# Four copies of 32 row-fetched tokens instead of three of 42, and weighed activations two pairs of tiles ahead

## The chip, the cores and the metric

The kernel runs on one core of one Trainium2 chip. Its time is the device time of one execution in microseconds (us). Each kernel is executed several times, and the median is compared.

## What is computed

The reference is one layer of a stream encoder on 272 tokens (16 learned ones and 256 of the input): a layer norm, two kinds of attention, an output projection, and at the end a feed-forward part (PEER) that holds two thirds of the time. For each of the 256 input tokens PEER picks 128 of 16384 one-neuron experts and sums them:

```
h = layer_norm(ALPHA * h + mix, ln1_g[l], ln1_b[l])
...
s1, i1 = lax.top_k(s[:, :, 0], P_TOPK)
s2, i2 = lax.top_k(s[:, :, 1], P_TOPK)
...
g = jax.nn.softmax(top, axis=-1).reshape(P_BLOCK, P_HEADS * P_TOPK)
act = jax.nn.gelu(jnp.einsum('td,tkd->tk', xb, u_tab[eidx]))
return jnp.einsum('tk,tkd->td', g * act, v_tab[eidx])
```

`u_tab` and `v_tab` are 16384 rows of 2048 numbers each, in float32: 134 MB per table, in HBM.

## The kernel before

PEER is done in two ways at once, and the tokens are divided between them. The **dense tokens** (NT = 214 of the 256) go through all 16384 experts on TensorE; experts that were not picked get the weight 0. The other NS = 42 tokens are **row-fetched**: for each expert that such a token picked, its row of the table is fetched by an indirect DMA, and VectorE does the sums. G = 3 copies of the 42 tokens stand on 126 partitions, and each copy takes a third of the 128 experts, so that K = 43 fetches of `u_tab` and 43 of `v_tab` (126 rows of 8 KB each, 1.03 MB) do for all of them.

The tables come in half tiles of 128 x 1024 (512 KB, called units here). `load_half` (line 128) puts a unit into one of four buffers `raw` from SyncE's queue (SP); `split_half` rounds it to `wh` on ScalarE (L134) and makes the remainder `wl` on VectorE (L137). There are four buffers of each. `begin()` starts the next unit, three ahead of the one that TensorE reads, and a unit's load waits until its buffer has been read by L137.

Stage **U** loops over 128 tiles of `u_tab` (two units each). Every tile makes 16 products for the dense tokens, each of two matmuls: 214 columns with `wl` (L1114) and 2 x 214 = 428 columns with `wh` (L1115); the first product of a tile has three (L1110 to L1112). After a tile, the generator `activation` takes its sum from PSUM in steps, four steps to a tile: a copy on ScalarE (L1055), a sum on VectorE (L1057), a pause, then the gelu on ScalarE (L1068 into `slots` for the first HELD = 74 tiles, L1073 into `ya` and from there to the DRAM array `ad` for the others). In the same stage GpSimd scatters the experts' weights into the DRAM array `gd` (L957, 256 indirect DMAs).

Stage **V** loops over the 128 tiles of `v_tab`, once for each half of the columns (h = 0, 1), one unit at a time, 8 products to a unit (`value`, same lines L1114 and L1115). Its moving operand is `wv`, the weighed activations of a pair of tiles, made by `weigh(i)` in three steps: times `gd` on VectorE (L1094), rounded on ScalarE (L1097), the remainder on VectorE (L1099). For h = 1 the first step is left out where the product is still in SBUF, for tiles up to `far` = HELD + LATE. While TensorE reads pair i, `weigh(i+1)` is issued at products 0, 3 and 6 of the pair's first unit. When it ends, `fetch_weights(i+2)` asks for the pair's part of `gd` (214 KB) on ScalarE's DMA queue, into the buffer (one of two) that was just read.

In both stages `sparse(rate)` lets the row-fetched tokens on: it adds 2 x rate to a credit, and each credit pays for one fetch (`fetch_row`, L1031, on GpSimd) or for one use of a fetched buffer (`use_row`: L1018 in the first table, L1025 in the second, on VectorE). Rates are 0.36 in U, once a tile from tile 28 on, and 0.2 in V, once a unit. There are two buffers, and each fetch waits until its buffer has been used.

TensorE, VectorE, ScalarE and SP work strictly in the order in which these loops are written; nothing reorders it in U and V.

Of the kernel before, what the change touches and what calls it, by code (L numbers as in the profile page):

```python
# [19 lines left out]
P = 128  # L20
# [4 lines left out]
L = NM + S  # L25
# [8 lines left out]

G = 3
NS = P // G
# [3 lines left out]

HELD, LATE = 74, 40

# [5 lines left out]
def hybrid_layer(ctx: ExitStack, tc: tile.TileContext, a: dict):  # L48
# [578 lines left out]
    def use_ckv(wh, wl):  # L627
        ps = project(wh, wl, hT, 0, L)
        hi = g.tile([P, L], F32R, name="ckh", tag="vwh", bufs=2)
        lw = g.tile([P, L], F32R, name="ckl", tag="vwl", bufs=2)  # L630
        nc.scalar.copy(out=hi, in_=ps)
        nc.vector.tensor_tensor(out=lw, in0=ps, in1=hi.bitcast(F32), op=ALU.subtract)
        ck.append((hi, lw))
        step()
# [426 lines left out]
    def activation(j, ps):  # L1061

        x = tmp()[:, :NT]
        yield from gather_out(two(ps), x)
        yield
        yield
        if j < HELD:
            nc.scalar.activation(out=slots[:, j], in_=x, func=AF.Gelu_apprx_tanh)  # L1068
            return
        k = (j - HELD) % 4  # L1070
        if k == 0:
            spill[:] = [g.tile([P, 4, NT], F32, name="ya", tag="wv", bufs=2)]
        nc.scalar.activation(out=spill[0][:, k], in_=x, func=AF.Gelu_apprx_tanh)  # L1073
        if k == 3 or j == P - 1:
            nc.scalar.dma_start(out=ad[:, j - HELD - k:j - HELD + 1], in_=spill[0][:, :k + 1])
# [13 lines left out]
    def weigh(i):  # L1089
        h, m = divmod(i, P // 2)  # L1090
        j = 2 * m
        x = slots[:, j:j + 2] if j < HELD else late[0][:, j - HELD:j - HELD + 2] if j < far else ring[m % 2]
        if h == 0 or j >= far:
            nc.vector.tensor_tensor(out=x, in0=x, in1=gts[m % 2], op=ALU.mult)  # L1094
            yield
        w = g.tile([P, 2, 2, NT], F32R, name="wv", bufs=2)
        nc.scalar.copy(out=w[:, :, 0], in_=x)  # L1097
        yield
        nc.vector.tensor_tensor(out=w[:, :, 1], in0=x, in1=w[:, :, 0].bitcast(F32), op=ALU.subtract)  # L1099
        wv[m] = w  # L1100
        fetch_weights(i + 2)
# [14 lines left out]

    def value(pv, wh, wl, j, d):
        ds_ = slice(d * P, (d + 1) * P)
        product(pv[d], wh[:, ds_], wl[:, ds_], wv[j // 2][:, j % 2], j == 0, j == P - 1)

# [54 lines left out]
    for n in range(2 * P):  # L1175
# [11 lines left out]
        for k in range(KT // 2):  # L1187
            kt, ks = i * KT // 2 + k, slice(k * P, (k + 1) * P)
            product(ps, wh[:, ks], wl[:, ks], hT[:, kt, :, :NT], kt == 0, kt == KT - 1)
            if k % 4 == 3:  # L1190
                q = 2 * i + k // 4
                if q == 3:
                    sparse(0.36 if j >= 28 else 0)
                if q == 3 or (q == 1 and (j % 8 or j < 28)):
                    scatter_some(1)
                step()
        if n == 2 * P - 2:
            whole_of(weigh(0))
    drain()
    whole_of(activation(P - 1, ps))  # L1200
    over = g.tile([P, KT * 2 * L], F32, name="over", tag="actT")
# [6 lines left out]
    for lo in range(0, LATE, 8):  # L1208
        later.append((16 + lo // 2, late[0][:, lo:lo + 8], ad[:, lo:lo + 8]))
    for t in range(2):  # L1210
# [7 lines left out]
    for h in range(2):  # L1218
        pv = [psum() for _ in range(8)]
        for j in range(P):  # L1220
# [8 lines left out]
            w = got.popleft()  # L1229
            if j % 2 == 0 and h * P + j < 2 * P - 2:  # L1230
                stage = weigh((h * P + j) // 2 + 1)
            for d in range(8):
                value(pv, *w, j, d)
                if j % 2 == 0 and d in (0, 3, 6) and stage:
                    next(stage, None)
                if d == 4:
                    sparse(0.2)
        if h == 0:
# [47 lines left out]
    for d in range(8):  # L1286
        value(pv, *w, P - 1, d)
        whole_of(gather_out(two(pv[d]), res[:, 8 + d, :NT]))
# [82 lines left out]
```

## Time and profile before

| | us |
|---|---|
| median of 3 runs (lowest to highest) | 2107.59 (2090.7 to 2110.59) |
| the profiled execution, its own time | 2106.06 |
| its span in the trace | 2104.3 |

The profile is of one execution; 1.8 us of its time lie outside the span. A busy time of PE (TensorE) is not TensorE at its peak: matmuls overlap, and an instruction's duration is longer than the distance to the next. Where a stage is to be priced, the distance of starts counts. "PEclk" is the granted clock as a share of 2.4 GHz; 1.2 GHz is the only other level. "DMA" is the mean busy share of 16 DMA engines.

### The profile page before, as it was taken

How to read it: one execution, taken by the hardware profiler on the slowest of the kernel's cores; microseconds unless marked ns; L12 is line 12 of the kernel's file. 1: busy time of each engine (PE TensorE's matmuls, PEld its weight loads, DVE VectorE, ACT ScalarE, POOL GpSimd, SP SyncE). 2: the span in 40 equal slices, each digit the busy share in tenths (PEclk: the TensorE clock that was granted, in tenths of full speed). 3: DMA queues.
4: the chain of work that ended last, by engine and by line, in shares of the span. 5: the costliest groups of instructions: out<-in, count | busy, mean ns of one | idle time of the engine just before them, and what ended most of it. 6: DMA issues, size and time to landing. Idle time of an engine off the chain costs nothing.

```text
span 2104.3 us, 32423 instructions
## 1 busy us (share of the span) xinstructions
PE 1910.5 (91%) x12376; PEld 1799.4 (86%) x12376; DVE 1463.7 (70%) x2193; ACT 976.0 (46%) x1458; POOL 676.5 (32%) x402
## 2 busy tenths in 40 slices
PE   7889998998999988999999998988999889998885
PEld 5888998887999978988989897878888779988784
DVE  7564577556879889756667665766777767766567
ACT  5443454534456555444545453444444445443432
POOL 3000003003588806777877673100100101101001
PEclk9999999999999999999999999999999989999997
DMA  6995443553768868999999999898888868899881
GB/s 191 272 251 178 161 159 137 181 191 122 210 181 207 210 205 244 263 251 261 288 280 298 259 310 283 284 321 277 297 294 295 293 226 279 282 294 267 274 293 52
DMA packets 186636, 506.08 MB, mean 241 GB/s; under 512 B 54534, under 2 KB 84366, under 8 KB 173838
## 3 DMA queue, kind: packets, MB, share of 16 engines
q1 hardware_dynamic: 115312, 370.96, 54.6%
q0 software_dynamic: 52256, 98.06, 19.5%
q10 hardware_dynamic: 18912, 34.99, 4.8%
q8 instruction: 97, 1.59, 0.3%
q14 instruction: 59, 0.48, 0.1%
HBM read 477.62 MB, written 25.16 MB: 239 GB/s over the span
## 4 chain that ended last, share of the span: by engine, by line
DMA 28%; PE 18%; DVE 15%; issue 8%; ACT 6%; ACTq 1%; POOL 0%; DVEq 0%; SPq 0%
DMA raw<-u_tab 14%; DMA raw<-v_tab 11%; PE ps L1115 9%; DVE wl L137 7%; ACT wh L134 5%; PE ps L1114 4%; DMA mem<-gd 2%; PE ps L181 1%; PE ps L180 1%; PE ps L179 1%; DVE tmp L1057 1%; DVE wv L1099 1%; DVE mem L1025 1%; DVE mem L1018 1%; DMA raw<-w_pq 1%
## 5 line engine op out<-in xcount | busy, mean ns | idle before, releaser
L137 DVE TENSOR_TENSOR wl<-raw,wh 128x1024 fp32r<-128x1024 f32 x660 | 809.0, 1231 | 490.7 <-ACT wh L134 473.4
L134 ACT CAST wh<-raw 128x1024 fp32r<-128x1024 f32 x666 | 695.4, 1049 | 734.1 <-DMA raw<-u_tab 195.0
L1115 PE MATMUL ps<-wv,wh 128*128 128x428 f32 x2032 | 658.5, 385 | 33.2 <-DVE wv L1099 33.0
L1115 PE MATMUL ps<-actT,wh 128*128 128x428 f32 x1920 | 606.0, 373 | 0.0
L1114 PE MATMUL ps<-wv,wl 128*128 128x214 f32 x2032 | 546.0, 269 | 40.5 <-ACT wv L1097 40.5
L1114 PE MATMUL ps<-actT,wl 128*128 128x214 f32 x1920 | 509.7, 265 | 26.7 <-DVE wl L137 26.6
L957 POOL DMA_INDIRECT gd<-mem x256 | 479.5, 1873 | 85.6 <-issue 75.3
L1115 PEld LDWEIGHTS ps<-wv,wh 128*128 128x128 f32 x2032 | 397.1, 195 | 58.6 <-DVE wv L1099 42.0
L1114 PEld LDWEIGHTS ps<-wv,wl 128*128 128x128 f32 x2032 | 404.1, 199 | 47.3 <-ACT wv L1097 47.2
L1114 PEld LDWEIGHTS ps<-actT,wl 128*128 128x128 f32 x1920 | 369.6, 193 | 33.6 <-DVE wl L137 33.2
L1115 PEld LDWEIGHTS ps<-actT,wh 128*128 128x128 f32 x1920 | 364.3, 190 | 14.7
L179 PE MATMUL ps<-actT,wh 128*128 128x256 f32 (+1 forms) x944 | 278.4, 295 | 4.9 <-ACT actT L350 4.9
L180 PE MATMUL ps<-actT,wh 128*128 128x256 f32 (+1 forms) x944 | 272.7, 289 | 4.6 <-POOL actT L229 4.4
L181 PE MATMUL ps<-actT,wl 128*128 128x256 f32 (+1 forms) x944 | 271.4, 288 | 0.5 <-DVE wl L137 0.5
L1031 POOL DMA_INDIRECT mem<-v_tab,mem x43 | 58.8, 1368 | 565.2 <-DVE mem L1025 506.7
L179 PEld LDWEIGHTS ps<-actT,wh 128*128 128x128 f32 x944 | 182.7, 194 | 12.6 <-ACT actT L350 5.2
L180 PEld LDWEIGHTS ps<-actT,wh 128*128 128x128 f32 x944 | 182.3, 193 | 7.4 <-POOL actT L229 6.1
L181 PEld LDWEIGHTS ps<-actT,wl 128*128 128x128 f32 x944 | 182.0, 193 | 0.7 <-DVE wl L137 0.7
L1031 POOL DMA_INDIRECT mem<-u_rows,mem x43 | 63.1, 1467 | 230.7 <-DVE mem L1018 201.3
L1097 ACT CAST wv<-mem 128x428 fp32r<-128x428 f32 x88 | 48.3, 548 | 124.0 <-DVE mem L1094 118.8
L1025 DVE SCALAR_TENSOR_TENSOR mem<-mem 126x2048 f32<-126x2048 f32 x42 | 98.5, 2346 | 0.0
L1018 DVE CUSTOM_DVE_ANT_0 mem<-mem 126x2048 f32<-126x2048 f32 x43 | 98.2, 2285 | 0.0
(281 smaller groups left out, 1634.7 us busy)
## 6 DMA issues: line engine op xcount, KB each, us to landing
raw<-u_tab SPq DMA_DIRECT2D x256, 512.0 KB
raw<-v_tab SPq DMA_DIRECT2D x256, 512.0 KB
raw<-w_in SPq DMA_DIRECT2D x86, 512.0 KB
raw<-w_out SPq DMA_DIRECT2D x32, 512.0 KB
raw<-w_pq SPq DMA_DIRECT2D x32, 512.0 KB
mem<-gd ACTq DMA_DIRECT2D x71, 214.0 KB
gd<-mem SPq DMA_DIRECT2D x16, 856.0 KB
ad<-ya ACTq DMA_DIRECT2D x13, 428.0 KB
```

The source lines that it names most:

```text
L134: acts.append(order(nc.scalar.copy(out=wh, in_=raw)))
L137: subs.append(order(nc.vector.tensor_tensor(out=wl, in0=raw, in1=wh.bitcast(F32), op=ALU.subtract)))
L179: nc.tensor.matmul(out, wh, ah, start=first, stop=False)
L180: nc.tensor.matmul(out, wh, al, start=False, stop=False)
L181: nc.tensor.matmul(out, wl, ah, start=False, stop=last)
L957: s = nc.gpsimd.indirect_dma_start(out=gdf[:, :], out_offset=bass.IndirectOffsetOnAxis(ap=idx, axis=0), in_=val, in_offset=None, compute_o ...
L1018: nc.vector.tensor_tensor_reduce(out=buf[:U], in0=buf[:U], in1=xsp[:U], scale=1.0, scalar=0.0, op0=ALU.mult, op1=ALU.add, accum_out=sact[: ...
L1025: nc.vector.scalar_tensor_tensor(out=xsp[:U], in0=buf[:U], scalar=sw[:U, k:k + 1], in1=xsp[:U], op0=ALU.mult, op1=ALU.add)
L1031: f = nc.gpsimd.indirect_dma_start(out=buf[:U], out_offset=None, in_=a["u_rows" if n < K else "v_tab"], in_offset=bass.IndirectOffsetOnAxi ...
L1097: nc.scalar.copy(out=w[:, :, 0], in_=x)
L1114: nc.tensor.matmul(lo, wl, x[:, 0], start=False, stop=False)
L1115: nc.tensor.matmul(two(ps)[:, :, :NT], wh, x, start=False, stop=last)
```

## The change

It does three things. First, G goes from 3 to 4: 32 tokens are row-fetched, on 4 x 32 = 128 partitions, 32 fetches per table, and 224 tokens are dense. HELD and LATE become 70 and 38 (the buffers' bytes), and the rates become 0.33 and 0.14. Second, `wv` has three buffers instead of two, is kept by the pair's running number i, and `weigh(i+2)` is issued where `weigh(i+1)` was; the first two pairs are weighed ahead of V. To make room, two small tiles of an early stage share the buffers of `wv`. Third, `activation` pauses for two steps more, half a tile, ahead of the gelu.

```
-G = 3
+G = 4
...
-HELD, LATE = 74, 40
+HELD, LATE = 70, 38
...
         yield from gather_out(two(ps), x)
-        yield
-        yield
+        for _ in range(4):
+            yield
...
-        w = g.tile([P, 2, 2, NT], F32R, name="wv", bufs=2)
+        w = g.tile([P, 2, 2, NT], F32R, name="wv", bufs=3)
...
-        wv[m] = w
+        wv[i] = w
...
-                    sparse(0.36 if j >= 28 else 0)
+                    sparse(0.33 if j >= 28 else 0)
...
         if n == 2 * P - 2:
             whole_of(weigh(0))
+        if n == 2 * P - 1:
+            whole_of(weigh(1))
     drain()
+    while beside:
+        step()
...
-            if j % 2 == 0 and h * P + j < 2 * P - 2:
-                stage = weigh((h * P + j) // 2 + 1)
+            if j % 2 == 0:
+                i = (h * P + j) // 2 + 2
+                stage = weigh(i) if i < P else None
...
-                    sparse(0.2)
+                    sparse(0.14)
```

On ScalarE (ACT), in the middle of U, one tile stood like this before (numbers are those of the buffers; the copy and the gelu of one tile have neighbouring `tmp` numbers):

```order
L1055 COPY tmp_13217<-ps_13151 128x214
L134 CAST wh_13230<-raw_13228 128x1024
L1073 ACTIVATE ya_13198<-tmp_13216 128x214
L134 CAST wh_13253<-raw_13251 128x1024
L1055 COPY tmp_13268<-ps_13206 128x214
```

and stands like this now:

```order
L1055 COPY tmp_13208<-ps_13142 128x224
L1073 ACTIVATE ya_13218<-tmp_13152 128x224
L134 CAST wh_13223<-raw_13221 128x1024
L134 CAST wh_13246<-raw_13244 128x1024
L1055 COPY tmp_13261<-ps_13197 128x224
L1073 ACTIVATE ya_13218<-tmp_13207 128x224
```

Before, the gelu of a tile (`tmp_13216`) stood behind the copy of the same tile (`tmp_13217`), one cast later; now it stands behind the copy of the next tile (`tmp_13207` behind `tmp_13261`), ahead of both casts.

On ScalarE at the end of U and the start of V, before:

```order
L1055 COPY tmp_13375<-ps_13309 128x214
L1097 CAST wv_13387<-mem_76 128x2x214
L1085 DMA mem_76<-gd_289 128x428
L134 CAST wh_13393<-raw_13391 128x1024
L1073 ACTIVATE ya_13413<-tmp_13374 128x214
L1055 COPY tmp_13416<-ps_13362 128x214
L1073 ACTIVATE ya_13413<-tmp_13415 128x214
L1075 DMA ad_290<-ya_13413 128x428
L134 CAST wh_13432<-raw_13430 128x1024
L1097 CAST wv_13449<-mem_76 128x2x214
```

and now:

```order
L1097 CAST wv_13382<-mem_76 128x2x224
L1085 DMA mem_76<-gd_289 128x448
L134 CAST wh_13388<-raw_13386 128x1024
L1097 CAST wv_13410<-mem_76 128x2x224
L1085 DMA mem_76<-gd_289 128x448
L1073 ACTIVATE ya_13414<-tmp_13367 128x224
L1055 COPY tmp_13417<-ps_13355 128x224
L1073 ACTIVATE ya_13414<-tmp_13416 128x224
L1075 DMA ad_290<-ya_13414 128x448
L134 CAST wh_13433<-raw_13431 128x1024
L1097 CAST wv_13450<-mem_76 128x2x224
```

One more pair is weighed ahead of the last tile's copy (L1055), so that the cast in V's first unit is that of the third pair and no longer of the second; from there on each is a pair earlier. The distance from a fetch of `gd` (L1085) to the cast behind the product that reads it is two pairs, as before.

On GpSimd (POOL) from the last scatters to the end of V, before:

```order
L957 DMA gd<-mem 4194304x1 x3
L1031 DMA mem<-u_rows,mem 126x2048 x8
L1031 DMA mem<-v_tab,mem 126x2048 x30
L1226 MEMSET mem 128x16x42
L1031 DMA mem<-v_tab,mem 126x2048 x13
```

and now:

```order
L957 DMA gd<-mem 4194304x1 x5
L1031 DMA mem<-v_tab,mem 128x2048 x27
L1230 MEMSET mem 128x16x32
L1031 DMA mem<-v_tab,mem 128x2048 x5
```

After the last scatter 51 fetches followed before, and 32 do now; all fetches of `u_rows` (the row layout of `u_tab`) stand between the scatters.

## Rows read from the trace of the kernel before

**Rows 1.** The page: the span, the busy times of the engines, and the DMA engines' busy share in 40 slices of the span, in tenths.

```profile
span 2104.3 us, 32423 instructions
PE 1910.5 (91%) x12376; PEld 1799.4 (86%) x12376; DVE 1463.7 (70%) x2193; ACT 976.0 (46%) x1458; POOL 676.5 (32%) x402
...
DMA  6995443553768868999999999898888868899881
```

**Rows 2.** The instructions of line 1110, the first matmul of a sum: 128 tiles of U, then 16 sums of V, with the first and last start.

```profile
L1110 PE MATMUL ps<-actT,wh x128: 261/261/381, 607.8 to 1293.4; 128*128 128x214 f32 x128
L1110 PE MATMUL ps<-wv,wh x16: 418/545/547, 1304.9 to 1706.9; 128*128 128x214 f32 x16
```

**Rows 3.** What TensorE waited for most in U (607 to 1305 us): total us, times, longest.

```profile
PE ps L1114 <- DVE wl L137: 26.6, 22, 3.6
```

**Rows 4.** What TensorE waited for in V (1305 to 2062 us), all of it.

```profile
PE ps L1114 <- ACT wv L1097: 40.5, 24, 5.6
PE ps L1115 <- DVE wv L1099: 33.0, 38, 1.9
PE ps L1110 <- DVE tmp L1057: 7.8, 8, 3.4
PE ps L1110 <- ACT wv L1097: 6.4, 1, 6.4
```

**Rows 5.** The table by stretches: length, busy us and instructions of PE, weight loads, VectorE, ScalarE and GpSimd, then the granted clock, the DMA share and GB/s. Four stretches of U, both halves of V, all of V, and one short stretch of V for PE's line 1115 alone.

```profile
607.00:700.00 93.00, 93.00 (x627) 90.71 (x626) 84.99 (x229) 54.58 (x87) 80.20 (x43) 1.00 0.80 199
700.00:850.00 150.00, 134.95 (x863) 127.76 (x861) 135.78 (x339) 80.40 (x134) 75.46 (x46) 0.99 0.80 225
850.00:1000.00 150.00, 140.00 (x904) 133.75 (x903) 97.04 (x105) 71.23 (x110) 111.00 (x61) 0.99 0.92 256
1000.00:1250.00 250.00, 240.24 (x1560) 231.23 (x1560) 163.42 (x175) 123.73 (x188) 192.91 (x108) 0.99 1.00 286
...
1305.00:1707.00 402.00, 351.30 (x2078) 330.54 (x2078) 285.64 (x301) 169.06 (x205) 34.34 (x26) 0.93 0.88 290
1707.00:2062.00 355.00, 324.18 (x1990) 310.50 (x1991) 242.43 (x220) 158.57 (x188) 33.46 (x24) 0.95 0.85 270
...
1305.00:2062.00 757.00, 675.47 (x4067) 641.05 (x4068) 528.08 (x521) 327.63 (x393) 67.79 (x50) 0.94 0.86 281
...
1350.00:1400.00 50.00, 40.94 (x132) 24.57 (x131) 0.98 0.98 323
```

**Rows 6.** The timeline of PE in V: the first and the last of 27 matmuls of line 1114 with no wait between them (start, us).

```profile
1480.10 0.26 PE L1114 MATMUL ps<-wv,wl 128*128 128x214 f32 x1
...
1488.08 0.26 PE L1114 MATMUL ps<-wv,wl 128*128 128x214 f32 x1
```

**Rows 7.** The chain of work in U: the second matmuls of two tiles that follow one another with no wait (start, us).

```profile
1103.16 0.11 PE ps L1111
...
1108.10 0.11 PE ps L1111
```

**Rows 8.** The timeline of PE in V, from a wait on.

```profile
1650.22 0.73 PE L1115 MATMUL ps<-wv,wh 128*128 128x428 f32 x1 [1.78 <-DVE wv L1099]
1650.74 0.38 PE L1114 MATMUL ps<-wv,wl 128*128 128x214 f32 x1
...
1651.32 0.38 PE L1114 MATMUL ps<-wv,wl 128*128 128x214 f32 x1
```

**Rows 9.** The timeline of PE in an early stage: the first and last of 36 matmuls of 256 columns, and of 74 of 272 columns, each with no wait between.

```profile
209.84 0.29 PE L180 MATMUL ps<-actT,wh 128*128 128x256 f32 x1
...
214.00 0.28 PE L179 MATMUL ps<-actT,wh 128*128 128x256 f32 x1
...
235.81 0.29 PE L179 MATMUL ps<-actT,wh 128*128 128x272 f32 x1
...
244.97 0.29 PE L180 MATMUL ps<-actT,wh 128*128 128x272 f32 x1
```

**Rows 10.** The page's groups of the remainder and the cast of a unit, and of the fetched rows' uses on VectorE, and from the table of lines from 570 us on that of the weighing's product: busy us in total, mean ns of one.

```profile
L137 DVE TENSOR_TENSOR wl<-raw,wh 128x1024 fp32r<-128x1024 f32 x660 | 809.0, 1231 | 490.7 <-ACT wh L134 473.4
L134 ACT CAST wh<-raw 128x1024 fp32r<-128x1024 f32 x666 | 695.4, 1049 | 734.1 <-DMA raw<-u_tab 195.0
...
L1025 DVE SCALAR_TENSOR_TENSOR mem<-mem 126x2048 f32<-126x2048 f32 x42 | 98.5, 2346 | 0.0
...
L1094 DVE TENSOR_TENSOR mem<-mem 128x428 f32<-128x428 f32 x51 | 30.5, 598 | 4.3 <-DMA mem<-gd 2.9 <-DMA mem<-ad 1.4
```

**Rows 11.** What the other engines waited for, in U (700 to 1330 us) the first two, in V (1330 to 2060 us) the others.

```profile
ACT wh L134 <- DMA raw<-u_tab: 193.3, 88, 6.3
ACT mem L1068 <- DVE tmp L1057: 53.1, 36, 3.3
...
ACT wh L134 <- DMA raw<-v_tab: 111.9, 62, 7.4
ACT wv L1097 <- DVE mem L1094: 107.4, 46, 4.3
```

**Rows 12.** The chain of work in V: transfers that it passes through (start, us from the step before to the landing).

```profile
1399.91 11.58 DMA mem<-gd
...
1491.42 10.46 DMA mem<-gd
...
1524.11 9.02 DMA raw<-v_tab
```

More of the change, by code (lines that the diff above doesn't have):

```diff
@@ L628, in use_ckv @@
         ps = project(wh, wl, hT, 0, L)
-        hi = g.tile([P, L], F32R, name="ckh", tag="vwh", bufs=2)
-        lw = g.tile([P, L], F32R, name="ckl", tag="vwl", bufs=2)
+        both = g.tile([P, 2, L], F32R, name="ckv", tag="wv", bufs=3)
+        hi, lw = both[:, 0], both[:, 1]
         nc.scalar.copy(out=hi, in_=ps)
@@ L1071, in activation @@
         if k == 0:
-            spill[:] = [g.tile([P, 4, NT], F32, name="ya", tag="wv", bufs=2)]
+            spill[:] = [g.tile([P, 4, NT], F32, name="ya", tag="wv", bufs=3)]
         nc.scalar.activation(out=spill[0][:, k], in_=x, func=AF.Gelu_apprx_tanh)
@@ L1115, in product, with value @@
             nc.tensor.matmul(two(ps)[:, :, :NT], wh, x, start=False, stop=last)
-    def value(pv, wh, wl, j, d):
+    def value(pv, wh, wl, j, d, h):
         ds_ = slice(d * P, (d + 1) * P)
-        product(pv[d], wh[:, ds_], wl[:, ds_], wv[j // 2][:, j % 2], j == 0, j == P - 1)
+        product(pv[d], wh[:, ds_], wl[:, ds_], wv[(h * P + j) // 2][:, j % 2], j == 0, j == P - 1)
     def affines():
@@ L1208, in hybrid_layer @@
     for lo in range(0, LATE, 8):
-        later.append((16 + lo // 2, late[0][:, lo:lo + 8], ad[:, lo:lo + 8]))
+        later.append((16 + lo // 2, late[0][:, lo:min(lo + 8, LATE)], ad[:, lo:min(lo + 8, LATE)]))
     for t in range(2):
@@ L1229, in hybrid_layer @@
             w = got.popleft()
-            if j % 2 == 0 and h * P + j < 2 * P - 2:
-                stage = weigh((h * P + j) // 2 + 1)
+            if j % 2 == 0:
+                i = (h * P + j) // 2 + 2
+                stage = weigh(i) if i < P else None
             for d in range(8):
-                value(pv, *w, j, d)
+                value(pv, *w, j, d, h)
                 if j % 2 == 0 and d in (0, 3, 6) and stage:
@@ L1286, in hybrid_layer @@
     for d in range(8):
-        value(pv, *w, P - 1, d)
+        value(pv, *w, P - 1, d, 1)
         whole_of(gather_out(two(pv[d]), res[:, 8 + d, :NT]))
```

## The prediction

> **What bounds the kernel now.** I read the page first: TensorE is busy for 91% of the span, VectorE for 70%, and the DMA engines are at 8 or 9 tenths from the middle on [rows 1]. Such shares mix stages, so I cut the span by the first matmuls of the tiles: U begins at 607.8 us, V at 1304.9 [rows 2], and V ends near 2062. U takes 697 us, V 757; what lies before (608) and behind (42) computes the same as now.
>
> Then I ask what each stage would take if TensorE never waited. In V 26 products take 7.98 us [rows 6], 0.307 us each, so that 2048 of them take 629 us. In U a tile of 16 takes 4.94 us [rows 7], and 128 tiles 632 us. So V loses 757 - 629 = 128 us and U 697 - 632 = 65.
>
> V's loss has a name. All that TensorE waits for there is the weighed operand, 40.5 + 33.0 us in the stage and 6.4 at its start, and 7.8 at the change of the banks [rows 4]: 88 us together. It never waits for `wl` or `wh`, which are ready. A wait costs more than its length: behind one of 1.78 us, two matmuls of line 1114 start 0.58 us apart and not 0.307 [rows 8]. Over V the granted clock is 0.94 [rows 5]. With x of the time at half speed, 1 - x/2 = 0.94 gives x = 0.12, 91 us in which half is lost: 45 us. 88 + 45 = 133 is the loss, within 5.
>
> Why is the operand late? ScalarE's cast waits 107 us for the product on VectorE [rows 11], which is queued behind `wl` of a unit that TensorE needs only three units later, and that one's cast waits for its transfer (112 us). So a transfer that has three units' time still delays the weighing, which has two.
>
> U is different. From 1000 to 1250 us the DMA engines are at 1.00 [rows 5] and ScalarE waits for `raw` (193 us, [rows 11]); 1560 instructions at 33 per tile are 47.3 tiles, 5.29 us each. From 850 to 1000 a tile takes 5.48 us. From 700 to 850 VectorE is busy for 90% of the time and 863/33 = 26 tiles take 5.7 us each. Only the first 19 tiles run at TensorE's pace. TensorE's own waits in U, 26.6 us at line 1114 [rows 3], are for `wl`.
>
> **The change, part by part.**
>
> *Wider matmuls.* A product goes from 214 + 428 to 224 + 448 columns, 30 more. No row has these widths. In an early stage 35 matmuls of 256 columns take 4.16 us, 0.1189 each, and 73 of 272 columns 9.16 us, 0.1255 each [rows 9]: 0.41 ns per column, 12.4 ns per product. If all of the 0.307 us grew with the columns, it would be 14.3 ns; with the slope of one short stretch, 10. I take 12.4: 2048 x 12.4 ns = 25 us in each stage (20 to 29). The floors become 654 us in V and 657 in U, a tile of U 5.14 us. The Trainium skill's page TensorE: Matmul & The Clock Gate, section Back-to-back issue gap, gives N/2.4 + 2.5 ns for a matmul alone. By it a product would take 272 ns now, which the measured 307 contradicts; its slope, 12.5 ns for 30 columns, would give 51 us for both stages against my 50.
>
> *Fewer rows.* The tables' row fetches fall from 86 of 1.03 MB to 64 of 1.05 MB, and VectorE loses 22 uses of 2.3 us [rows 10], 51 us that lay beside TensorE's work. What counts is where the fetches stand. GpSimd's entries in V now are 26 + 24, less one that clears memory [rows 5]: 49 fetches, 50.6 MB. By the order 32 are left behind the last scatter, 33.6 MB. V moves 757 us x 281 GB/s = 213 MB [rows 5]. It will move 213 - 51 + 34 + 2 (wider `gd` and three more pairs of the late tiles) = 198 MB. In U a tile moves 1.05 MB of table, 0.36 x 1.03 of rows and 0.06 of `ad`, 1.48 MB; with 0.33 x 1.05 it is 1.46, 1.5% less.
>
> *Two pairs ahead.* The three steps of `weigh` stand where they stood, for a pair that is needed two units (about 5 us) later. The longest wait was 5.6 us, and the mean of the 62 inside V 1.2 us [rows 4], so these 74 us go, and most of the clock's 45. The third buffer is the one of the pair just finished, so the cast waits for TensorE no longer than now. The fetch of `gd` keeps its distance of two pairs: no more lead there. At V's start the second pair's weighing now stands ahead of the last tile's copy; the copy frees the last PSUM bank, wanted 7 products (2.2 us) into V, and the weighing takes about 1.7 us on two engines. I price this at nothing to 4 us.
>
> *What is late next in V.* With the weighing out of the way, TensorE next needs `wl` in time, that is, the transfers. At V's mean rate 198 MB take 198 / 0.281 = 705 us; at the best stretch's 323 GB/s [rows 5] 613 us, below the floor of 654. The page DMA: Bandwidth & Descriptors of the Trainium skill, section Where 436 GB/s comes from, puts a core's HBM limit at about 358 GB/s, 553 us; no stretch here shows that rate. I take the floor, 14 us at the two transitions (6.4 + 7.8 as now), 15 of the clock, and 17 of new waits, nearer to the mean rate than to the best one: 654 + 46 = 700 us, 57 less. Bounds: 670 (floor and transitions) to 757.
>
> *The gelu later, and U.* Before, ScalarE stood at the gelu until VectorE had made the tile's sum, 53 us in total [rows 11], with the next cast behind it. Now it does what was ready a tile ago. This helps where `wl` is late and costs nothing; it gives between 0 and TensorE's 27 us of waits [rows 3]. Against it stands the wider matmul: 19 tiles at TensorE's pace pay 0.2 us each, 4 us; in the other tiles the floor of 5.14 us stays below the 5.29 to 5.7 that transfers and VectorE set. Where the DMA engines are at 1.00, 1.5% fewer bytes over some 300 us give 4 us. I take 5 us for the gelu, of the 0 to 27 nearer to nothing since most of ScalarE's waiting is for transfers: 697 + 4 - 4 - 5, U ends at 692, 5 less. Bounds: 660 to 722 (the widening paid in full).
>
> **The sum.** The profiled execution took 2106.06 us, 2104.3 in its span and 1.8 outside, close to the median of 2107.59. 2106 - 57 - 5 = 2044; with the 2 us midway of V's start 2046. I say 2046.
>
> **The rivals.**
>
> *The fetch of `gd` becomes V's pace.* From one weighing to the next but one lie the product, 0.6 us [rows 10], and the landing, 10.46 us in one place and 11.58 in another [rows 12]: with their mean of 11.0, 11.6 us for two pairs. At the new floor two pairs take 10.2 us. If the landing stays, the first half, where every pair needs `gd`, takes 32 x 11.6 + 14 = 385 us, against 327 + 14 + 16 = 357 in my forecast: 28 more, 2074 us. For it: the chain passes through such landings. Against: they are its worst, and the queues that they share carry less. The wait would now stand on VectorE, with several us of lead behind it. Its point: a mean landing over 9.6 us.
>
> *U pays for the columns in full.* If TensorE's waits in U come on top of the longer products and do not shrink by them, U becomes 722 us, 30 more than in my forecast: 2076. For it: waits come in groups, so that some tiles run at the floor even from 1000 us on. Against: the DMA engines at 1.00 set that stretch's mean.
>
> *Slower: the ring of four `raw` buffers sets V's pace.* A buffer's round is the landing, the cast and the remainder (1.05 + 1.23 us, [rows 10]), and must fit into four units. If landings rise to a mean of 10 us, a unit takes 12.3 / 4 = 3.07 us, V 256 x 3.07 + 14 = 800 us and the kernel 2106 + 43 - 5 = 2144. It decides against the change from a landing of 9.4 us on (2.92 us a unit, 748 + 14 = 762 us). For it: 9.02 us in the chain [rows 12]. Against: that is one of the chain's long ones, TensorE never waits for `wl` in V today though V runs at 281 GB/s, and the bytes fall by 7%.
>
> **How the numbers follow.** 60% for the forecast (2046, its own range 2015 to 2075), 18% for the `gd` fetch (2074; 2093 if every landing takes 11.58 us), 14% for U's columns (2076; 2062 to 2095), 8% for slower (2144). The range from 2000 to 2093 leaves out the slower case and some 10% of the others; its lower end takes V at 675 us and U at 675. About 1% is what a measurement of this kernel tells from no change; faster by more than that means below 2086. The forecast holds nearly all of its 60% there, the two middle rivals 17 of their 32, so faster 0.77, same 0.16, slower 0.07.
>
> **What would show it.** In the profile after: TensorE's waits for line 1097 and 1099 nearly gone in V, a granted clock near 0.98 there, V near 700 us; the distance of products 0.319 us; 32 fetches in V; no ScalarE waits at the gelu. Wrong would be: TensorE waiting for `wl` (L137) in V for over 50 us, VectorE's L1094 waiting for `gd` for tens of us, or tiles of U longer than 5.5 us from 1000 us on.

## The result, and the profile after

The changed kernel takes 1960.65 us (median of 4 runs, 1960.09 to 1967.57) against 2108.28 us before (4 runs, 2090.7 to 2110.59): a ratio of 0.932, 95% interval 0.927 to 0.938. The forecast was 2046, with a range of 2000 to 2093. The direction was right; the gain is 148 us and not some 60, and the time lies 39 us below the range. The profiled execution took 1960.09 us, 1958.3 of them in its span. Of the two runs of e13 below, one fell into the chip's slower state; the time given for e13 is the other's.

The page after, against [rows 1]:

```profile
span 1958.3 us, 32249 instructions
PE 1873.9 (96%) x12376; PEld 1761.0 (90%) x12376; DVE 1418.1 (72%) x2163; ACT 977.0 (50%) x1458; POOL 668.2 (34%) x381
...
DMA  6974444364667787899999999799888867779882
```

TensorE is busy for 96% of the span in place of 91%. The same first matmuls as in [rows 2] cut the span into stages:

```profile
L1110 PE MATMUL ps<-actT,wh x128: 262/263/370, 589.7 to 1234.5; 128*128 128x224 f32 x128
L1110 PE MATMUL ps<-wv,wh x16: 272/415/556, 1242.6 to 1602.4; 128*128 128x224 f32 x16
```

| stretch | before, us | after, us | forecast | measured |
|---|---|---|---|---|
| ahead of U | 608 | 590 | 0 | -18 |
| U | 697 | 653 | -5 | -44 |
| V (ends near 2062, now near 1916) | 757 | 673 | -57 | -84 |
| behind V | 42 | 42 | 0 | 0 |

So the three stretches ahead of the tail all gained, and the two in which little or nothing was forecast gave 62 of the 146 us. What TensorE waited for over the whole span, the longest rows, against [rows 3, 4]:

```profile
PE ps L1114 <- DVE wl L137: 16.5, 22, 1.9
PE ps L1110 <- DVE tmp L1057: 11.1, 9, 3.6
PE ps L328 <- DVE bnst L217: 7.6, 1, 7.6
...
PE ps L1110 <- ACT wv L1097: 3.0, 1, 3.0
```

The waits for the weighed operand at lines 1114 and 1115 are gone, as forecast. But the waits for `wl` at line 1114 have shrunk too, to 16.5 us over the whole span from 26.6 in U alone, where the sum had the later gelu give 5. The table by stretches (columns as in [rows 5]; U, then V's two halves, then 200 us of U's late part):

```profile
590.00:1242.60 652.60, 642.62 (x4231) 616.61 (x4229) 506.99 (x874) 356.20 (x557) 491.44 (x267) 1.00 0.90 270
1242.60:1602.00 359.40, 337.10 (x2077) 315.33 (x2077) 269.61 (x285) 166.68 (x205) 33.12 (x18) 0.97 0.87 307
1602.00:1916.00 314.00, 312.60 (x1979) 297.47 (x1979) 218.02 (x209) 157.20 (x184) 20.68 (x13) 0.99 0.79 275
...
1000.00:1200.00 200.00, 199.52 (x1321) 192.24 (x1319) 134.94 (x146) 104.00 (x160) 156.18 (x86) 1.00 0.96 297
```

From 1000 to 1200 us U runs at TensorE's own pace: 1321/33 = 40 tiles of 5.00 us. Before, a tile took 5.29 us from 1000 to 1250 us, with the DMA engines at 1.00 and 286 GB/s [rows 5]. Now they are at 0.96 and move 297 GB/s. More bytes in a second at a lower share: the transfers themselves became cheaper.

### The profile page after: what moved, and what is told of

It is laid out like the page before. It is cut to its first block, busy times and chain, and to the rows that moved or that the text cites. A ratio compares the mean times of both kernels' runs of the same rounds, so it can differ in the third digit from the quotient of the medians.

```text
span 1958.3 us, 32249 instructions
## 1 busy us (share of the span) xinstructions
PE 1873.9 (96%) x12376; PEld 1761.0 (90%) x12376; DVE 1418.1 (72%) x2163; ACT 977.0 (50%) x1458; POOL 668.2 (34%) x381
## 3 DMA queue, kind: packets, MB, share of 16 engines
q0 software_dynamic: 47712, 76.41, 15.0%
## 4 chain that ended last, share of the span: by engine, by line
PE 49%; DVE 10%; DMA 6%; issue 4%; ACT 4%; ACTq 0%; POOL 0%; DVEq 0%
PE ps L1115 29%; PE ps L1114 15%; DVE wl L137 4%; DMA raw<-v_tab 3%; ACT wh L134 2%; DMA raw<-u_tab 2%; PE ps L181 1%; PE ps L180 1%; PE ps L179 1%; DVE mem L1025 1%; DVE mem L1094 1%; DVE wv L1099 1%; PE ps L1112 1%; PE ps L1111 1%; ACT wv L1097 1%
## 5 line engine op out<-in xcount | busy, mean ns | idle before, releaser
L1115 PE MATMUL ps<-wv,wh 128*128 128x448 f32 x2032 | 643.2, 376 | 0.0
L1115 PE MATMUL ps<-actT,wh 128*128 128x448 f32 x1920 | 603.7, 370 | 0.0
L1114 PE MATMUL ps<-wv,wl 128*128 128x224 f32 x2032 | 541.9, 267 | 12.2 <-DVE wl L137 12.1
L1114 PE MATMUL ps<-actT,wl 128*128 128x224 f32 x1920 | 511.1, 266 | 5.3 <-DVE wl L137 4.4
L1115 PEld LDWEIGHTS ps<-wv,wh 128*128 128x128 f32 x2032 | 383.9, 189 | 29.0
L1114 PEld LDWEIGHTS ps<-wv,wl 128*128 128x128 f32 x2032 | 390.5, 192 | 18.0 <-DVE wl L137 17.9
L1097 ACT CAST wv<-mem 128x448 fp32r<-128x448 f32 x90 | 50.8, 564 | 123.7 <-DVE mem L1094 121.1
L1099 DVE TENSOR_TENSOR wv<-mem,wv 128x448 fp32r<-128x448 f32 x90 | 56.1, 623 | 31.0 <-ACT wv L1097 31.0
L1031 POOL DMA_INDIRECT mem<-u_rows,mem x32 | 50.5, 1577 | 71.0 <-DVE mem L1018 57.6
L1018 DVE CUSTOM_DVE_ANT_0 mem<-mem 128x2048 f32<-128x2048 f32 x32 | 73.1, 2285 | 0.0
```

The source lines that it names most:

```text
L1018: nc.vector.tensor_tensor_reduce(out=buf[:U], in0=buf[:U], in1=xsp[:U], scale=1.0, scalar=0.0, op0=ALU.mult, op1=ALU.add, accum_out=sact[: ...
L1031: f = nc.gpsimd.indirect_dma_start(out=buf[:U], out_offset=None, in_=a["u_rows" if n < K else "v_tab"], in_offset=bass.IndirectOffsetOnAxi ...
L1114: nc.tensor.matmul(lo, wl, x[:, 0], start=False, stop=False)
L1115: nc.tensor.matmul(two(ps)[:, :, :NT], wh, x, start=False, stop=last)
```

## The experiments

Times are medians; the ratios are to the kernel before on the same chip, with 95% intervals. The first four do one or two parts of the change alone. e6 and e7 have one run each and no interval. The runs were on several chips, on which the kernel before has medians from 2106.56 to 2119.28 us: a difference of some 10 us between two runs is not told by their times alone.

### The gelu later, alone (e1)

```diff
-        yield
-        yield
+        for _ in range(4):
+            yield
```

(and the remainder of the activations is run to its end behind the last tile.)

> The kernel before with the third part of the change alone (the gelu half a tile later; 42 tokens on three copies, weighing one pair ahead). If ScalarE's standing at the gelu is what held U back, U falls from 697 us to 670 or less, V stays at 757, and the time is about 2080. If U was held by its transfers (rows of 214 numbers, fetches from 126 partitions), U stays at 685 to 697 and the time at 2095 or more. The stretch ahead of U stays at 608 us by either.

2107.01 us, 0.9968 (0.9942 to 0.9993). In the old kernel this part is worth some 0.3%, if that; in its trace U still takes 700 us, from 620 to 1321.

### Two pairs ahead, alone (e2), and with the gelu (e3)

```diff
-        w = g.tile([P, 2, 2, NT], F32R, name="wv", bufs=2)
+        w = g.tile([P, 2, 2, NT], F32R, name="wv", bufs=3)
...
+        if n == 2 * P - 1:
+            whole_of(weigh(1))
...
-            if j % 2 == 0 and h * P + j < 2 * P - 2:
-                stage = weigh((h * P + j) // 2 + 1)
+            if j % 2 == 0:
+                i = (h * P + j) // 2 + 2
+                stage = weigh(i) if i < P else None
```

> The kernel before with the second part alone (three buffers for the weighed activations, two pairs ahead). If V's loss was the wait for the weighed operand, as the prediction has it, V falls from 757 us to 690 or less, U stays at 697 and the time is about 2040. If V was held by transfers, TensorE waits for wl instead, V stays above 730 and the time above 2080.

> The second and the third part without the first (still 42 tokens on three copies, 214 dense). By the prediction's price of the wider matmuls (50 us) this would be as fast as the whole change or faster: about 1960 to 2000. If 224 columns and 32 tokens bring something themselves (cheaper transfers, no dearer matmuls), it lies 40 us or more above the whole change, over 2000.

e2: 2113.26 us, 0.9997 (0.9955 to 1.0039). e3: 2105.45 us, 0.9989 (0.9953 to 1.0025). The part on which the forecast put most of its gain is worth nothing by itself that these runs can tell; V takes 742 us in e2's trace (from 1312.8 us), where 690 or less was expected of it. Where the gain went, TensorE's waits in e2 from 1300 us on, and ScalarE's in V:

```profile
PE ps L1114 <- DVE wl L137: 64.7, 54, 5.1
PE ps L1110 <- DVE tmp L1057: 11.4, 8, 6.6
PE ps L1110 <- ACT wv L1097: 5.7, 1, 5.7
```

```profile
ACT wh L134 <- DMA raw<-v_tab: 164.5, 87, 7.1
```

The 73.5 us of waits for the weighed operand [rows 4] became 64.7 us of waits for `wl`, of which V before had none; and the cast behind `wl` waits 164.5 us for its transfer, where it waited 112 [rows 11]. The weighing was the first thing to be late, not the thing that set the pace. That was V's transfers.

### 32 tokens on four partitions each, alone (e4)

```diff
-G = 3
+G = 4
...
-HELD, LATE = 74, 40
+HELD, LATE = 70, 38
...
-                    sparse(0.36 if j >= 28 else 0)
+                    sparse(0.33 if j >= 28 else 0)
...
-                    sparse(0.2)
+                    sparse(0.14)
```

> The first part alone: 32 tokens in four copies, 224 dense, with the buffers and rates that go with it; weighing one pair ahead in two buffers, the gelu where it was. By the prediction's prices (50 us for the columns, 15 MB less in V) the time stays within 2085 to 2125 and the stretch ahead of U at 608 us. If rows of 224 numbers make the transfers cheaper, the stretch ahead of U falls to about 590 us as in the changed kernel, U to 670 or less, and the time to 2050 or less.

1980.25 us, 0.938 (0.9345 to 0.9418): 133 of the 148 us. This one number changes several things at once: the fetches' number (43 to 32 a table), their partitions (126 to 128), the width of a product (214 to 224), and with it the length of a row of `gd` and `ad` (856 to 896 bytes). The next runs take these apart.

### Only `gd`'s rows longer (e5)

The kernel before, with `gd`'s rows at a distance of 224 numbers, of which 214 are used.

```diff
+NTP = 224
...
-    gdf = dram.tile([P * P * NT + NS * P * P, 1], F32, name="gd")
+    gdf = dram.tile([P * P * NTP + NS * P * P, 1], F32, name="gd")
...
-        z = mem[:, 10048:10048 + NT]
+        z = mem[:, 10048:10048 + NTP]
```

> The kernel before, with 224 numbers instead of 214 kept for each token row of the DRAM array gd (896 bytes instead of 856; the last 10 are zeros that nobody uses): the zeroing, the scatters' addresses and the fetches of gd use the wider rows, 42 tokens stay row-fetched, 214 dense. If rows of 856 bytes were what slowed the transfers, the stretch ahead of U falls from 608 us to about 590 and V below 700, the time to 2000 to 2060. If the 126 partitions or the number of row fetches did it, nothing changes outside 1% (2090 to 2125).

2093.70 us, 0.9937 (0.9907 to 0.9967), 13 us. U starts at 595.3 us, 12.5 earlier than before; it starts at 608 to 620 us in the five traces with rows of 856 bytes and at 584 to 595 in those with 896. The gain lies where `gd` is cleared, 16 writes from SyncE's queue. From 50 to 100 us, first the kernel before, then e5:

```profile
50.00:100.00 50.00, 44.63 (x338) 43.16 (x337) 25.25 (x23) 22.69 (x33) 1.50 (x2) 0.94 1.08 276
```

```profile
50.00:100.00 50.00, 49.27 (x403) 48.19 (x401) 30.45 (x28) 27.79 (x41) 1.50 (x2) 1.00 1.00 327
```

276 GB/s became 327, though the array is 5% larger in e5, and the changed kernel has nearly the same row (326 GB/s). In the traces' packet records the 16384 packets of these writes take 65 ns each in the mean with 856 bytes and 42 with 896. Whether it is the length of a row or where its start lies (896 is a multiple of 128, 856 is not) was not separated.

### Only the fetches on 128 partitions (e11)

The kernel before, with 43 + 43 fetches as ever, each of 128 rows; the last two partitions fetch row 0, which is not used.

```diff
-        f = nc.gpsimd.indirect_dma_start(out=buf[:U], out_offset=None, in_=a["u_rows" if n < K else "v_tab"], in_offset=bass.IndirectOffsetOnAxis(ap=srow[:U, n % K:n % K + 1], axis=0))
+        f = nc.gpsimd.indirect_dma_start(out=buf, out_offset=None, in_=a["u_rows" if n < K else "v_tab"], in_offset=bass.IndirectOffsetOnAxis(ap=srow[:, n % K:n % K + 1], axis=0))
```

> The kernel before, with each row fetch on 128 partitions instead of 126 (the last two fetch row 0 and nobody uses them); everything else, and the uses on 126 partitions, as before. If 126 partitions spread badly over the 16 DMA engines, U falls from 697 us to 665 or less and V below 710, the time to 2000 to 2060. If not, the time stays within 1% of before.

2007.95 us, 0.9543 (0.9499 to 0.9587): 99 us, by fetching more. This is the largest single cause, and no part of the forecast's sum had it. It lies in both stages:

```profile
L1110 PE MATMUL ps<-actT,wh x128: 261/261/381, 617.4 to 1262.5; 128*128 128x214 f32 x128
L1110 PE MATMUL ps<-wv,wh x16: 418/545/548, 1271.0 to 1647.2; 128*128 128x214 f32 x16
```

U takes 654 us in place of 697. V, which ends near 1970, takes 699 in place of 757: what the forecast wanted of the earlier weighing came without it, and TensorE's waits for the weighed operand at lines 1114 and 1115 fell from 73.5 us to 36.7. From 1000 to 1200 us in e11:

```profile
1000.00:1200.00 200.00, 200.00 (x1339) 195.07 (x1338) 141.41 (x151) 105.54 (x160) 167.74 (x89) 1.00 0.99 308
```

TensorE is busy throughout, and the DMA engines move 308 GB/s at a share of 0.99, where they moved 286 at 1.00 [rows 5]. What is different shows in the queue of the row fetches (its packets, MB, and their time as a share of 16 engines' span), first before, then e11:

```profile
q0 software_dynamic: 52256, 98.06, 19.5%
```

```profile
q0 software_dynamic: 50880, 99.46, 17.9%
```

1.4 MB more in 1376 fewer packets: 16 packets fewer a fetch, although each has two rows more. A row is one packet (the counts of the next section), so the fetch of 126 rows has 18 that are no row. The rows' own packets became quicker, too: by the packet records one takes 446 ns in the mean before and 352 in e11.

### The reverse, and other numbers of partitions (e8, e12, e13, e16, e17)

The changed kernel, its fetches and their uses cut to fewer partitions; what the experts on the partitions left out would add is missing.

```diff
-    U = G * NS
+    U = G * NS - 2
```

(-2 in e8, -16 in e12, -4 in e13, -64 in e16, -32 in e17.)

> The changed kernel with row fetches and uses on 126 of the 128 partitions (a quarter of the experts of two tokens is left out). The counterpart: if 126 partitions are the cause, U rises from 653 us to 690 or more and V from 676 to 720 or more, the time to 2030 or more. If not, it stays at 1960, within 1%.

> The changed kernel with row fetches and uses on 112 of the 128 partitions (half of the fourth copy's experts are left out): 7 rows for each of 16 DMA engines. If what matters is that the rows divide evenly by 16, it is as fast as the changed kernel, 1945 to 1965 us, though 126 rows took 2031. If any number under 128 costs, it is at 2010 or more.

> The changed kernel with row fetches and uses on 124 of the 128 partitions. If a fetch is spread over the largest number of engines up to 16 that divides its rows, 126 ran on 14 and 124 run on 4: far slower than 126, 2100 us or more. If the rest over a multiple of 16 is what costs (14 rows of 126, 12 of 124), it is like 126, 2020 to 2045 us.

> The changed kernel with row fetches and uses on 64 of 128 partitions (the third and fourth copies' experts are left out), 4 rows for each of 16 engines. If rows that fall in groups of four partitions are quick (128 and 64, but not 112 with seven to an engine), the mean time of a packet of the GpSimd queue is as with 128 and the time is at most 1960. If any number under 128 costs, it stays above 1970 though half of the bytes are gone.

> The same on 96 of 128 partitions, 6 rows for each of 16 engines. If groups of four matter, 96 costs like 112: 1990 to 2010 us with three quarters of the bytes. If 112 was slow for a reason of its own, 96 is at most 1960.

| rows a fetch | us | ratio, 95% | packets of q0 | share of q0 | ns of a row's packet |
|---|---|---|---|---|---|
| 128 (the change) | 1960.65 | 0.9324 (0.927 to 0.9379) | 47712 | 15.0% | 351 |
| 126 (e8) | 2031.33 | 0.9683 (0.9631 to 0.9734) | 48736 | 15.6% | 415 |
| 124 (e13) | 2613.89 | 1.24 | 71264 | 14.1% | 486 |
| 112 (e12) | 2010.68 | 0.9522 (0.9465 to 0.958) | 46688 | 15.7% | 460 |
| 96 (e17) | 1989.97 | 0.9435 (0.9377 to 0.9493) | 45664 | 15.2% | 497 |
| 64 (e16) | 1977.25 | 0.9375 (0.9314 to 0.9435) | 43616 | 13.1% | 560 |

Two rows fewer cost 71 us (V took 690 us in e8, less than the 720 expected); four fewer cost 653. (1.24 is 2613.89, a single run, over 2112.26, the median before on that chip.) The last column is the mean over the 8 KB packets of that queue from U's start on, in each trace's packet records; in number they are just the rows that the fetches asked for. The packet counts say how a fetch was split. With 112, 96 and 64 rows the count falls by just the rows left out, 64 times. With 126 it has 18 more a fetch than rows, with 124 it has 372. These are 2 x 9 and 12 x 31: if 14 engines carry nine rows each, 2 idle engines get nine empty packets; if 4 engines carry 31, 12 get 31. The page counts them, too, as packets under 512 bytes (first the changed kernel, then e13):

```profile
DMA packets 183293, 488.80 MB, mean 250 GB/s; under 512 B 52553, under 2 KB 83537, under 8 KB 173137
```

```profile
DMA packets 206844, 486.80 MB, mean 186 GB/s; under 512 B 76360, under 2 KB 107344, under 8 KB 196944
```

23807 more of them, 372 for each of 64 fetches. The Trainium skill's page DMA: Bandwidth & Descriptors, section Why a DMA increments its semaphore by 16 and not by 1, states the rule: a transfer is spread over the largest number of engines up to 16 that divides the slowest dimension of both its sides (some direct copies from GpSimd's queue are excepted), so 128 and 96 rows go over 16. By it 126 gives 14 and 124 gives 4, which these counts agree with. The section doesn't name fetches by index. By its rule 64, 96 and 112 rows go over all 16 engines as 128 do, and one would expect them to cost no more. They do cost more (17, 29 and 50 us), with a longer packet for each row (560, 497 and 460 ns against 351), and the expectations that built on the rule alone failed.

### Places in SBUF (e19), and half rows on all partitions (e18)

e19 fetches 64 whole rows, as e16 does, but onto every second partition. e18 fetches 128 half rows, as many bytes as e16, on all partitions. In both, other rows stand beside the weights than the layer asks for, so that only the times are of use; both clear the two buffers once.

```diff
+        if n < 2:
+            nc.vector.memset(buf, 0.0)
...
-        f = nc.gpsimd.indirect_dma_start(out=buf[:U], out_offset=None, in_=a["u_rows" if n < K else "v_tab"], in_offset=bass.IndirectOffsetOnAxis(ap=srow[:U, n % K:n % K + 1], axis=0))
+        f = nc.gpsimd.indirect_dma_start(out=buf[::2], out_offset=None, in_=a["u_rows" if n < K else "v_tab"], in_offset=bass.IndirectOffsetOnAxis(ap=srow[:64, n % K:n % K + 1], axis=0))
```

(e18: `out=buf[:U, :D // 2]`, from the table seen as twice as many rows of half the length.)

> The changed kernel with each of its 64 row fetches taking the first or second half of a row (4 KB) on all 128 partitions: as many bytes as the fetch of whole rows on 64 partitions (1977 us), and every partition written. What the experts of the row-fetched tokens add is left out in part (only half of each row arrives). If what slows the fetches on 64, 96 and 112 partitions is that they leave partitions out, this one is at least as fast as the changed kernel: 1945 to 1962 us. If a smaller fetch does not speed the kernel up whatever its shape, and something else of these kernels costs 17 us, it lies at 1970 to 1985.

> The changed kernel with each row fetch of 64 whole rows, put on every second of the 128 partitions instead of the first 64; the other half of the rows, and with it the experts of two of the four copies, is left out. Same rows, packets and bytes as the fetch on the first 64 partitions (1977 us); only the places in SBUF differ. If the crowding of a fetch into the first half of the partitions costs the 17 us, it falls to 1945 to 1965 us; if the number of partitions written costs it, it stays at 1970 to 1985.

e18: 1951.72 us (1949.57 to 1952.70), 0.9242 (0.9167 to 0.9317). e19: 1956.77 us (1953.23 to 1962.76), 0.9279 (0.9201 to 0.9356). The ratios' intervals overlap with that of e16, which ran on another chip (1973.65 to 1980.85 us), so the times alone don't settle it. The traces do. The fetches' queue and ScalarE's wait for V's transfers, first e16, then e19:

```profile
q0 software_dynamic: 43616, 42.86, 13.1%
...
ACT wh L134 <- DMA raw<-v_tab: 81.2, 44, 6.7
```

```profile
q0 software_dynamic: 43616, 42.86, 11.6%
...
ACT wh L134 <- DMA raw<-v_tab: 12.4, 13, 2.4
```

Same packets, same bytes, and 13.1% of 1979 us against 11.6% of 1951: the same rows cost 13% less time on the DMA engines when they lie over the whole of SBUF, and the other transfers stop being late. A row's packet takes 375 ns in e19 and 560 in e16. Traces of the same fetches scatter far less: in the changed kernel and the five runs that fetch as it does (e4, e6, e7, e14, e15) the queue's share is 14.8 to 15.2%. So 64 rows cost time by being crowded into the first half of the partitions, not by their number. The Trainium skill's same page, section The descriptor swizzle, has each engine write a port of its own in a transfer to 128 partitions. That is a reason why other shapes could collide; no run here shows which engine wrote which partition. For 96 and 112 rows other places were not tried.

e18 also bears on the price of bytes. It moves 33.6 MB less than the changed kernel and is 9 us faster: an estimate of some 0.27 us for one MB, but from a difference that is no larger than that between chips.

### The number of fetches (e9)

The changed kernel with 43 + 43 fetches and the old rates; the last 11 of each table are fetched and used again without weight.

```diff
+    KF = 43
...
-                    sparse(0.33 if j >= 28 else 0)
+                    sparse(0.36 if j >= 28 else 0)
...
-                    sparse(0.14)
+                    sparse(0.2)
```

> The changed kernel with 43 fetches and uses per table instead of 32, at the rates of before (0.36 and 0.2); the last 11 of each table repeat earlier ones and add nothing to the output. If the 22 fewer fetches (23 MB) are the cause, V rises from 676 us to 740 or more and the time to 2030 or more. If they are not, the time stays below 1985.

1986.06 us, 0.944 (0.9397 to 0.9483), 25 us more than the change: between the two expectations, just above the 1985 of the lower one. From 1000 to 1200 us:

```profile
1000.00:1200.00 200.00, 200.00 (x1326) 192.98 (x1326) 140.06 (x150) 105.04 (x161) 164.91 (x90) 1.00 0.99 314
```

U still runs at TensorE's pace, at 314 GB/s with the DMA share at 0.99. What the 22 further fetches cost lies mostly in V, which takes 699 us against 673 (U 660 against 653), and where `wl` was waited for 31.2 us.

### Narrower products (e6, e7)

The changed kernel, all but the first product of a sum on 214 (e6) or 208 (e7) of its 224 columns; the tokens of the other columns miss their terms.

```diff
+NC = 214
...
-            nc.tensor.matmul(lo, wl, x[:, 0], start=False, stop=False)
-            nc.tensor.matmul(two(ps)[:, :, :NT], wh, x, start=False, stop=last)
+            nc.tensor.matmul(lo[:, :NC], wl, x[:, 0, :NC], start=False, stop=False)
+            nc.tensor.matmul(two(ps)[:, :, :NC], wh, x[:, :, :NC], start=False, stop=last)
```

> The changed kernel, but every product after the first of a sum reads and writes only the first 214 of the 224 columns (10 tokens miss 15 of 16 or 127 of 128 terms of their sums). In stretches without waits a tile of U (4.96 us) and a product of V (0.3115 us) show the price of 30 columns. At 0.41 ns per column, as predicted, U's tile falls to 4.77 and V's product to 0.299. If the array is fed in steps of 16 columns, U's tile stays at 4.94 to 4.96, since 214 and 224 fill the same 14 steps.

> The same with 208 of the 224 columns, 48 fewer per product. At 0.41 ns per column: a tile of U 4.65 us. In steps of 16 (13 instead of 14 for each of three rows): 48 columns at 0.417 ns are 20 ns per product, a tile of U again 4.65 us. So both theories agree here, and differ in the 214 of the run beside it.

1951.94 and 1950.66 us. Line 1115 alone in 210 us of V without waits, the changed kernel, then e6, then e7 (PE's busy us and matmuls, then weight loads). In e6 and e7 the lines stand one lower, so that their 1115 is the matmul with `wl`; it too comes once a product, and the counts are what is compared:

```profile
1640.00:1850.00 210.00, 210.00 (x672) 125.72 (x671) 1.00 0.82 288
```

```profile
1640.00:1850.00 210.00, 178.91 (x685) 130.83 (x686) 1.00 0.83 293
```

```profile
1640.00:1850.00 210.00, 179.99 (x701) 133.79 (x701) 1.00 0.85 300
```

A product takes 210/672 = 0.3125 us, 0.3066 on 214 columns and 0.2996 on 208. The 30 columns from 214 cost 5.9 ns and not 12.4; the 18 from 208 to 214 cost 7.0 (one matmul more or less in a count is 0.5 ns). Neither a straight line nor steps of 16 columns fit all three. In U, from 950 to 1050 us without waits, e6 has 670 matmuls and the changed kernel 664. At 33 to a tile that is 4.93 us in place of 4.97, 2.8 ns a product; at the predicted price 4.77 was expected. For e7 both theories had 4.65; from 900 to 1000 us (675 matmuls, 0.7 us idle) its tile takes some 4.89. With 208 columns the weight loads are busy for 199.50 of 200 us:

```profile
1650.00:1850.00 200.00, 200.00 (x1335) 199.50 (x1334) 148.14 (x138) 106.57 (x126) 17.32 (x11) 1.00 0.84 298
```

### The change without one of its parts (e14, e15)

e14 puts the gelu back to its earlier place, e15 the weighing to one pair ahead and two buffers.

```diff
-        for _ in range(4):
-            yield
+        yield
+        yield
```

```diff
-        w = g.tile([P, 2, 2, NT], F32R, name="wv", bufs=3)
+        w = g.tile([P, 2, 2, NT], F32R, name="wv", bufs=2)
...
-        if n == 2 * P - 1:
-            whole_of(weigh(1))
...
-            if j % 2 == 0:
-                i = (h * P + j) // 2 + 2
-                stage = weigh(i) if i < P else None
+            if j % 2 == 0 and h * P + j < 2 * P - 2:
+                stage = weigh((h * P + j) // 2 + 1)
```

> The changed kernel without its third part (the gelu where it was before). On the old transfers the gelu alone brought 0.3%. If it pays only once transfers are quick, the time rises from 1960 to 1968 or more; if the weighing holds all of what separates the first part alone (1980) from the whole change (1960), it stays at 1960 to 1964.

> The changed kernel without its second part (two buffers, one pair ahead). On the old transfers two pairs ahead brought nothing, since TensorE then waited 92 us for wl. With quick transfers, the 22 us that the first part alone still waits for the weighed operand, with the clock that goes with it, should come back: 1975 to 1985. If it too is idle here, the time stays within 1958 to 1965.

1967.82 us, 0.9335 (0.929 to 0.938), and 1968.11 us, 0.9341 (0.9294 to 0.9388): 7 us each, below the difference that the intervals can tell, though the runs of both (1967.45 to 1974.70) lie at or above nearly all of the change's. e15 lies between its two expectations. Without either, e4 is at 1980. TensorE's waits in e15:

```profile
PE ps L1115 <- DVE wv L1099: 14.5, 29, 1.8
PE ps L1110 <- DVE tmp L1057: 9.1, 9, 4.0
PE ps L1114 <- ACT wv L1097: 7.6, 8, 2.1
```

With quick transfers the weighed operand at one pair ahead costs 22 us of waits and not 73.5. Most of its lateness, too, came from the transfers.

## Why the prediction was wrong

**V's loss.** The step that failed is "V's loss has a name": from "all that TensorE waits for there is the weighed operand" it went to "these 74 us go". They went, and nearly as many came at `wl` (e2: 64.7, and V 742 us). The prediction had itself traced the late operand back to `wl` of another unit and to that one's transfer; it then removed the last link of this chain and counted the whole of it. Its "slower" rival, the ring of `raw` buffers setting V's pace, comes nearest to what e2 runs into, at an even price and not a loss: the casts wait for their transfers there. Whether it is the ring that holds those up, and not the DMA engines, no run shows. That V in the changed kernel fell by 84 us, past the 57 forecast, is no support for the step: e11 brought V to 699 us with the weighing as it was.

**Fewer rows.** The second step that failed, and the dearer: the fetches were priced by bytes ("1.5% less" in U, 198 MB for 213 in V), and their going from 126 rows to 128 had no term. Half of the fetched bytes are worth some 9 us (e18, across two chips). What counted is a fetch's shape: by the packet counts 126 rows go over 14 engines and 128 over 16, and a row's packet takes 446 ns before and 352 in e11. That is 99 us in the kernel before (e11), and 71 as the last step to the changed one (e8). From 86 fetches to 64 gave 25 (e9). It is this step that took the time out of the range: e8, the change on 126 partitions, takes 2031 us, with U at 703 and V at some 690 where the forecast has 692 and 700:

```profile
L1110 PE MATMUL ps<-actT,wh x128: 262/263/388, 589.2 to 1279.3; 128*128 128x224 f32 x128
L1110 PE MATMUL ps<-wv,wh x16: 274/484/556, 1292.0 to 1667.6; 128*128 128x224 f32 x16
```

That e8 comes within 15 us of the forecast is partly luck: the columns were priced some 41 us too dear, and the stretch ahead of U gained what had no term.

**U.** "The DMA engines at 1.00 set that stretch's mean" held before, but was read as a limit of bytes at 286 GB/s, so that only 1.5%, 4 us, could be had there. e11 and e9 have 308 and 314 GB/s at 0.99. A busy share of 1.00 said that the engines were occupied, not that they moved what they can. U's lower bound of 660 us rested on the wider matmul's floor; U took 653.

**The columns.** The mechanism was right, the term too large: 12.4 ns a product, taken from the early stages [rows 9], against 5.9 in V (e6); in U a tile takes 4.98 to 4.99 us (954.70, 959.68, 964.67) where it took 4.94 [rows 7], 2.8 ns a product. By e6, one run on another chip, the whole term is some 9 us and not 50:

```profile
954.70 0.11 PE ps L1111
...
959.68 0.11 PE ps L1111
964.67 0.11 PE ps L1111
```

The Trainium skill's section that the prediction named, Back-to-back issue gap of TensorE: Matmul & The Clock Gate, also states spacings for matmuls in a stream with their weight loads, 81 ns at 128 columns and 131 at 512. That slope of 0.13 ns a column would give an estimate of 3.9 ns for 30 columns, nearer to both readings than the formula for a matmul alone. The spacings themselves are not borne out: between them lies an estimate of 216 ns for matmuls of 224 and 448 columns, and a product takes 312.

**What lies ahead of U.** "Computes the same as now" was no reason to put it at nothing: it also clears `gd`, whose rows became 40 bytes longer, and that gave 13 us (e5). The prediction counted these bytes as a cost, within 2 MB in V.

**What was right.** The waits for lines 1097 and 1099 are nearly gone in V, the clock there is 0.97 and 0.99 in the two halves, ScalarE waits 10.2 us at the gelu and not 53, VectorE waits 0.3 us for `gd`, and V has no long wait for `wl` (12.1 us from 1200 us on). The rivals with `gd`'s fetch and with U's columns did not come about. Two of the change's three parts pay only some 7 us each, if that, once the transfers are quick (e14, e15), and nothing or little while they are not (e1 to e3).

**The sum.** From the runs: longer rows of `gd` -13 (e5), 128 partitions -99 (e11), fewer fetches -25 (e9), ahead and gelu -20 (e4 against the change), columns +9 (e6): -148, as measured. It is one order of taking the parts, from runs on several chips; the fetches' partitions alone are 99 or 71 by the side from which they are taken, so that the exact agreement is partly luck.

**What stays open.** Which part of the 126-row fetch's price is the two engines left out, and which the longer packet of each row (415 to 446 ns against some 350); why that packet is longer in every shape tried but 128 rows and every second partition, and whether that is what 96 and 112 rows cost by; whether the length or the start of `gd`'s rows counts; and why 30 columns cost less than half of the early stages' slope. No version that computes all of it was faster than the changed kernel.

## What to carry to other kernels

When an operand is late because of a chain that ends in a transfer, removing the chain's last link can move the wait to the next operand, as in e2; first ask what the transfers' pace would allow without it. Look at how each transfer is split before counting its bytes: compare the queue's packets with the rows that were asked for, and give a fetch 128 rows, two of them dummies if need be. A change of a size (here one number, three to four copies) changes every array that has it as a dimension: list them all, with the length of a row in bytes, ahead of the sum.

## What the runs showed of the hardware that was not expected

- A fetch by index of 124 rows made the kernel take 2614 us, one of 126 rows 2031, one of 128 rows 1961. The empty packets (372 and 18 a fetch) agree with 4 and 14 engines in use.
- With fetches of 64 rows of 8 KB, their queue took 13.1% of the 16 engines' time on the first 64 partitions and 11.6% on every second one, and the kernel 1977 and 1957 us on two chips. A row's packet took 560 and 375 ns.
- Clearing a DRAM array with rows of 896 bytes in place of 856 raised 276 GB/s to 327 in the same 50 us.
- A DMA share of 1.00 at 286 GB/s was followed by 314 GB/s at 0.99 in the same loop, with no fewer fetches.
